# A streaming-encoder layer on eight cores: channel-major data, interleaved stages, streamed weights, shifted-stack convolution, pow on GpSimd, list scheduling

## The chip, the cores and the metric

The kernel runs on all 8 cores of one Trainium2 chip (two dies, cores 0 to 3 and 4 to 7). Each core does the same program on its own four prompt sequences and its own share of sample streams; no core waits for another. The metric is device time in microseconds (us) of the slowest core. TensorE is called PE, VectorE DVE, ScalarE ACT, GpSimd POOL and SyncE SP, as in the profile.

A program on all 8 cores has a second, slower state in some of its executions: one die (sometimes both) shows a lower granted clock and the time is some per cent longer.

## The reference, cut to what matters

```python
# D_MODEL 1024, 2048 tokens per prompt sequence, D_FF 2816 = 22*128, D_LRU = D_CONV = 512
def stream_layer(x, c, ...):
    sh1, sc1, gt1, ... = silu(c) @ w_ada + b_ada               # per-sequence modulation
    h = rms_norm(x, g1) * (1 + sc1) + sh1
    x = x + 0.5 * gt1 * ((silu(h @ wg1) * (h @ wu1)) @ wd1)    # FFN1
    h = rms_norm(x, g2) * (1 + sc2) + sh2
    z_lx, z_lg, z_cv, z_cg = split(h @ w_in)                   # 1024 -> 4 x 512
    # group A: width-4 causal conv, RG-LRU recurrence, GeLU gate
    y = causal_dwconv4(z_lx)
    r, i = sigmoid(blockdiag(y, wa)), sigmoid(blockdiag(y, wx))
    log_a = -8.0 * r * softplus(-lambda)
    a = exp(log_a)
    b = sqrt(-expm1(2 * log_a)) * (i * y)                      # sqrt(1 - a^2) * i * y
    lru = scan(h_t = a_t * h_{t-1} + b_t) * gelu(z_lg)
    # group B: GLU, depthwise conv of width 31, LayerNorm, SiLU
    v = silu(layer_norm(causal_dwconv31(z_cv * sigmoid(z_cg))))
    x = x + gt2 * (concat(rms_norm(lru), rms_norm(v)) @ w_out)
    h = rms_norm(x, g3) * (1 + sc3) + sh3
    x = x + 0.5 * gt3 * ((silu(h @ wg2) * (h @ wu2)) @ wd2)    # FFN2
    return rms_norm(x, final_g), states
```

Per core this is 16 tiles of 512 prompt tokens and one sample tile of 128 tokens.

The element-wise powers are a reciprocal square root for each of seven norms per tile (RMSNorm before each of three sub-layers, the LayerNorm, two group norms, the final norm), and, for each of four channel blocks of the recurrence, one exponential `a` and one square root.

## The kernel before

It has three phases, each over all tiles: FFN1 with its bf16 weights resident in SBUF, the mixer, FFN2 with its weights loaded once more. Tokens lie on partitions in the FFN input, so each tile is transposed on PE.

```python
def fe_normb(...):                       # norm of 128 tokens; tokens on partitions
    act.activation(out=xq, in_=xb, func=AF.Square, accum_out=stat[:, b])       # sum of squares
    act.activation(out=stat[:, 4+b], in_=stat[:, b], func=AF.Sqrt, scale=1/D, bias=eps)
    dve.reciprocal(out=stat[:, 8+b], in_=stat[:, 4+b])          # one value per token: [128, 1]
    dve.tensor_scalar(out=xq, in0=xb, scalar1=stat[:, 8+b], op0=ALU.mult)
# ... cut ...
for k in range(8): pe.transpose(out=PSB[..k..], in_=xq[..k..])                 # L547
# ... cut ...
for j in range(22):                                                            # FFN
    for k in range(8): pe.matmul(PS[gb], lhsT=Wg[:, k, j], rhs=hT[:, k])       # L660
    for k in range(8): pe.matmul(PS[ub], lhsT=Wu[:, k, j], rhs=hT[:, k])       # L664
# ... cut: SiLU on ACT, product on DVE; the down projection is L691 ...

# the mixer's recurrence, per channel block c of 128 channels, 512 tokens
act.activation(out=BD, in_=tr, func=AF.Exp, scale=der3, bias=der3)             # a
act.activation(out=BC, in_=tr, func=AF.Exp, scale=der2, bias=der2)             # a^2
act.activation(out=BC, in_=BC, func=AF.Sqrt, scale=-0.25, bias=0.25)           # sqrt(1 - a^2)/2
# the depthwise conv of width 31: 31 diagonal 128x128 matrices per channel block
for k in range(31):
    pe.matmul(PS[bank], lhsT=D31[:, c, k, :], rhs=CU[:, c, k:k+512])           # L1011
# the group norm
act.activation(out=RS, in_=PS[6], func=AF.Sqrt, scale=1/512, bias=4*eps)
dve.reciprocal(out=RS, in_=RS)
# ... cut ...
```

Of the kernel before, what the change touches and what calls it, by code (L numbers as in the profile page):

```python
# [16 lines left out]
SEQ = 2048  # L17
DSEQ = 32
PSEQ_PER_CORE = 4
SSEQ_PER_CORE = 4  # L20
NPT = PSEQ_PER_CORE * SEQ
NST = SSEQ_PER_CORE * DSEQ
NSEQ = 8
EPS = 1e-6
NT = 512

class _FakeIns:
    def then_inc(self, *a, **k):
        return self

# [9 lines left out]

def _fsz(ap):
    sh = ap.shape
    n = 1
    for d in sh[1:]:
        n *= int(d)
    return n

def _cost(eng, rec):
    name, a, kw = rec
    out = kw.get('out', a[0] if a else None)  # L50
    try:
        n = _fsz(out) if out is not None else 1
    except Exception:
        n = 1
    if name == 'dma_start':
        try:
            nbytes = out.size() * (2 if out.dtype == BF16 else 4)
        except Exception:
            nbytes = 1 << 16
        return 2500.0 + nbytes / 150.0  # L60
    if eng == 'pe':
        if name == 'transpose':
            return 160.0
        rhs = kw.get('rhs')
        nn = _fsz(rhs)
        mul = 4.0 if rhs.dtype == F32 else 1.0
        return max(nn, 64) / 2.4 * mul + 4.0
    if eng == 'act':
        return 230.0 + 0.96 * n + (190.0 if kw.get('accum_out') is not None else 0.0)
    if eng == 'dve':  # L70
        if name == 'reciprocal':
            return 100.0 + 6.1 * n
        if name == 'tensor_tensor_scan':
            return 70.0 + 2.0 * n
        if name in ('tensor_tensor', 'scalar_tensor_tensor'):
            return 70.0 + 1.3 * n
        if name == 'memset':
            return 60.0 + 0.5 * n
        return 60.0 + 1.0 * n
    if eng == 'pool':  # L80
        if name == 'tensor_tensor':
            return 100.0 + 2.4 * n
        if name == 'memset':
            return 100.0 + 1.0 * n
        return 100.0 + 3.5 * n
    return 30.0

def _tbl(rec):
    name, a, kw = rec
    if name != 'activation':  # L90
        return None
    f = kw.get('func')
    if f in (AF.Sqrt,):
        return 'sqrt'
    if f in (AF.Tanh, AF.Exp):
        return 'tanhexp'
    if f in (AF.Silu,):
        return 'silu'
    if f in (AF.Ln,):
        return 'ln'  # L100
    return None

class Sched:
    ENGS = ['pe', 'act', 'dve', 'pool', 'sp']
    WINDOW = 700

    def __init__(self):
        self.ops = []
        self.lastw = {}
        self.readers = {}  # L110
        self.region = 0
        self.reorder = {0: True}

    def barrier(self, reorder=True):
        self.region += 1
        self.reorder[self.region] = reorder

    def add(self, eng, fn, reads=(), writes=(), slot=None):
        idx = len(self.ops)
        deps = {}  # L120
        for r in reads:
            w = self.lastw.get(r)
            if w is not None:
                deps[w] = True
        for r in writes:
            w = self.lastw.get(r)
            if w is not None:
                deps.setdefault(w, False)
            for rd in self.readers.get(r, ()):
                deps.setdefault(rd, False)  # L130
        keep = []
        alld = []
        for d, raw in deps.items():
            o = self.ops[d]
            if o['region'] != self.region:
                continue
            alld.append(d)
            if o['slot'] is None and o['eng'] == eng and slot is None and eng == 'pe':
# [4 lines left out]
        rec = fk.rec  # L143
        op = dict(eng=eng, fn=fn, deps=keep, alld=alld, slot=slot, val=None, used=False, region=self.region,
                  cost=_cost(eng, rec), tbl=_tbl(rec), idx=idx)
# [10 lines left out]
    def schedule(self):  # L156
        ops = self.ops
        nreg = self.region + 1
        byreg = [[] for _ in range(nreg)]
        for o in ops:  # L160
            byreg[o['region']].append(o['idx'])
        order = {e: [] for e in self.ENGS}
        regend = []
        tfree = {e: 0.0 for e in self.ENGS}
        fin = {}
        lasttbl = [None]
        for r in range(nreg):
            ids = byreg[r]
            t0 = max(tfree.values()) if r > 0 else 0.0
            for e in self.ENGS:  # L170
                tfree[e] = max(tfree[e], t0)
            ndep = {i: len(ops[i]['alld']) for i in ids}
            users = {i: [] for i in ids}
            for i in ids:
                for d in ops[i]['alld']:
                    users[d].append(i)
            ready = {e: [] for e in self.ENGS}
            pos = 0
            done = set()
            for i in ids:  # L180
                if ndep[i] == 0:
                    ready[ops[i]['eng']].append(i)
            nsched = 0
            ntot = len(ids)
            strict = ['sp'] if self.reorder.get(r, True) else list(self.ENGS)
            elist = {e: [i for i in ids if ops[i]['eng'] == e] for e in strict}
            eptr = {e: 0 for e in strict}
            idpos = {i: k for k, i in enumerate(ids)}
            while nsched < ntot:
                while pos < ntot and ids[pos] in done:  # L190
                    pos += 1
                lim = ids[min(pos + self.WINDOW, ntot - 1)] if pos < ntot else 0
                best = None
                for e in self.ENGS:
                    lst = ready[e]
                    if not lst:
                        continue
                    cands = lst
                    if e in eptr:
                        el = elist[e]  # L200
                        while eptr[e] < len(el) and el[eptr[e]] in done:
                            eptr[e] += 1
                        if eptr[e] >= len(el) or el[eptr[e]] not in lst:
                            continue
                        cands = [el[eptr[e]]]
                    for i in cands:
                        if i > lim:
                            continue
                        o = ops[i]
                        st = tfree[e]  # L210
                        for d in o['alld']:
                            if fin[d] > st:
                                st = fin[d]
                        pen = 0.0
                        if e == 'act' and o['tbl'] is not None and lasttbl[0] is not None and o['tbl'] != lasttbl[0]:
                            pen = 1300.0
                        key = (st + pen, i)
                        if best is None or key < best[0]:
                            best = (key, i, st, pen)
                if best is None:  # L220
                    allr = [i for e in self.ENGS for i in ready[e]]
                    i = min(allr)
                    o = ops[i]
                    st = tfree[o['eng']]
                    for d in o['alld']:
                        st = max(st, fin[d])
                    best = ((st, i), i, st, 0.0)
                _, i, st, pen = best
                o = ops[i]
                e = o['eng']  # L230
                ready[e].remove(i)
                if o['slot'] is not None:
                    tfree[e] = st + 60.0
                    fin[i] = st + o['cost']
                else:
                    if e == 'act' and o['tbl'] is not None:
                        lasttbl[0] = o['tbl']
                    tfree[e] = st + pen + o['cost']
                    fin[i] = tfree[e] + (200.0 if e == 'pe' else 60.0)
                order[e].append(i)  # L240
                done.add(i)
                nsched += 1
                for u in users[i]:
                    ndep[u] -= 1
                    if ndep[u] == 0:
                        ready[ops[u]['eng']].append(u)
            regend.append({e: len(order[e]) for e in self.ENGS})
        self.order = order
        self.regend = regend
        self.makespan = max(tfree.values())  # L250

    def emit(self, nc, stack):
# [7 lines left out]
        nreg = len(self.regend)  # L260
        for r in range(nreg):
            for e in engs:
                lo = self.regend[r - 1][e] if r > 0 else 0
                hi = self.regend[r][e]
                for k in range(hi - 1, lo - 1, -1):
                    o = ops[order[e][k]]
                    if o['slot'] is None:
                        o['used'] = True
                        break
        cnt = {e: 0 for e in engs}  # L270
# [905 lines left out]
```

## Time and profile before

| | before |
|---|---|
| time, median of 4 fast runs | 6520.56 us (6518.27 to 6533.39) |
| busy share PE / DVE / ACT / POOL | 82% / 36% / 35% / 14% |
| PE per 512-token FFN tile | 124.5 us for 528 matmuls |
| mixer phase | about 2200 us |

The first fence is from the profile's page: busy us, share of the span and instructions of each engine; then the span in 40 equal slices with the busy share of each in tenths (9 is 90% or more) and the granted PE clock in tenths.

```profile
PE 5315.6 (82%) x25588; PEld 2434.9 (37%) x25588; DVE 2323.1 (36%) x3919; ACT 2311.6 (35%) x4040; POOL 917.2 (14%) x855
...
PE   3699999999999747657757766756999999999998
...
POOL 0100010010001122222222222221100100010010
PEclk7899999999999978878878877867999999999999
```

There are two plateaus of nines with a valley between them: the FFN phases keep PE full, the mixer phase does not. The next view cuts the span at the phase borders (range, length, busy us and instructions of PE, PE's weight loads, DVE, ACT, POOL, granted PE clock, busy share of the DMA engines, GB/s).

```profile
0.00:342.50 342.50, 180.81 (x801) 79.15 (x802) 63.90 (x155) 48.70 (x86) 47.55 (x63) 0.77 0.85 133
342.50:2218.00 1875.50, 1774.58 (x8360) 815.48 (x8359) 444.59 (x804) 455.96 (x799) 150.45 (x119) 0.96 0.15 51
2218.00:4420.00 2202.00, 1422.89 (x7066) 638.82 (x7064) 1223.04 (x1860) 1145.93 (x1893) 534.25 (x511) 0.79 0.16 53
4420.00:4587.00 167.00, 124.52 (x593) 58.29 (x594) 42.78 (x86) 51.78 (x99) 29.54 (x40) 0.85 0.88 158
4587.00:6519.00 1932.00, 1812.76 (x8772) 843.19 (x8770) 548.74 (x1015) 609.27 (x1163) 155.39 (x123) 0.96 0.15 51
```

In the third row no engine is full, PE is at 65% and DVE at 56%, which fits a mixer that waits for its own chain. The first and the fourth row are mostly weight loads, with the DMA engines at 0.85 and 0.88 and PE busy 53% and 75%. So the change has a fair target: fill the mixer's holes and the load times with FFN matmuls.

How fast PE runs is read from the timeline (start us, us, engine, line, operation, names, shapes, count, and in brackets the idle time before and what ended it).

```profile
342.48 1.89 PE L660 MATMUL ps<-hT,Wg 128*128 128x512 bf16 x8
344.21 1.89 PE L664 MATMUL ps<-hT,Wu 128*128 128x512 bf16 x8
...
418.45 0.61 PE L547 MATMUL ps<-identb,xnb_0 128*128 128x128 bf16 x8
418.90 0.61 PE L547 MATMUL ps<-identb,xnb_1 128*128 128x128 bf16 x8
423.23 1.01 PE L547 MATMUL ps<-identb,xnb_2 128*128 128x128 bf16 x8 [3.72 <-DVE hT L563]
```

From start to start, eight matmuls take 344.21 − 342.48 = 1.73 us, so 216 ns for each 128x512 matmul. (The duration in the second column includes the tail of the pipeline; take the distance of starts.)

### The profile page before, as it was taken

The page shows a single profiled execution, that of the slowest core. Times are in us where ns is not written, and L with a number is a line of the kernel's source. Part 1 is how long each engine was busy: PE and PEld are TensorE (multiplying, and loading weights), DVE is VectorE, ACT ScalarE, POOL GpSimd, SP SyncE. Part 2 cuts the span into 40 slices and gives each one's busy share as a digit, 9 for nine tenths or more (in the row PEclk, how much of TensorE's full clock was granted, in tenths as well). Part 3 has the DMA queues.
Part 4 walks back from the last instruction along what each step waited for, and adds up shares of the span by engine and source line. Part 5 has one row for each costly group of instructions (what it writes and reads, how often), then busy time and mean ns, then how long its engine had stood idle before and what let it go on. Part 6 is the DMA issues. An engine that isn't in the chain of part 4 may idle for free.

```text
span 6518.4 us, 79218 instructions; the slowest of 8 cores (6502.7 to 6518.4 us)
## 1 busy us (share of the span) xinstructions
PE 5315.6 (82%) x25588; PEld 2434.9 (37%) x25588; DVE 2323.1 (36%) x3919; ACT 2311.6 (35%) x4040; POOL 917.2 (14%) x855
## 2 busy tenths in 40 slices
PE   3699999999999747657757766756999999999998
PEld 1344444444444423323323322332444444444444
DVE  1222222222222245565555565552222222232222
ACT  0222212222222145555554554542333332333332
POOL 0100010010001122222222222221100100010010
PEclk7899999999999978878878877867999999999999
DMA  8811111111111121111111111108111111111111
GB/s 120 149 65 46 43 65 52 43 53 64 43 46 62 47 61 63 51 46 67 47 46 52 59 49 48 60 27 152 65 52 43 52 65 43 43 66 52 39 56 43
DMA packets 141438, 381.75 MB, mean 59 GB/s; under 512 B 12808, under 2 KB 55944, under 8 KB 141016
## 3 DMA queue, kind: packets, MB, share of 16 engines
q1 hardware_dynamic: 87432, 316.77, 14.1%
q0 software_dynamic: 53600, 59.91, 6.4%
q8 instruction: 213, 3.49, 0.2%
q14 instruction: 193, 1.58, 0.1%
HBM read 333.44 MB, written 103.09 MB: 67 GB/s over the span
## 4 chain that ended last, share of the span: by engine, by line
PE 75%; DVE 7%; ACT 6%; issue 5%; DMA 5%; POOL 0%; DVEq 0%; ACTq 0%; POOLq 0%; SPq 0%
PE ps L691 20%; PE ps L660 18%; PE ps L664 18%; PE ps L1011 7%; PE ps L885 6%; PE ps L1079 3%; ACT hT L558 2%; DMA wslab<-w_ada 2%; DVE hT L563 1%; PE ps L547 1%; ACT hTm L558 1%; DMA Wu<-wu 1%; DVE hTm L563 1%; DMA Wd<-wd 1%; DVE BE L1036 1%
## 5 line engine op out<-in xcount | busy, mean ns | idle before, releaser
L660 PE MATMUL ps<-hT,Wg 128*128 128x512 bf16 (+1 forms) x5984 | 1361.9, 371 | 20.5 <-DVE hT L563 14.0
L664 PE MATMUL ps<-hT,Wu 128*128 128x512 bf16 (+1 forms) x5984 | 1359.9, 370 | 0.0
L691 PE MATMUL ps<-Wd,aT 128*128 128x512 bf16 x5720 | 1303.5, 392 | 14.9 <-DVE tmp_0 L694 8.9
L691 PEld LDWEIGHTS ps<-Wd,aT 128*128 128x128 bf16 x5720 | 575.2, 101 | 730.2 <-issue 100.0
L660 PEld LDWEIGHTS ps<-hT,Wg 128*128 128x128 bf16 x5984 | 574.1, 98 | 688.2 <-issue 29.1
L664 PEld LDWEIGHTS ps<-hT,Wu 128*128 128x128 bf16 x5984 | 574.3, 98 | 666.1 <-issue 2.9
L885 PE MATMUL ps<-hTm,Win 128*128 128x512 bf16 (+1 forms) x2176 | 650.7, 389 | 134.8 <-DVE hTm L563 100.9
L668 ACT ACTIVATE sg_0<-ps 128x512 bf16<-128x512 f32 (+1 forms) x374 | 216.3, 578 | 1304.9 <-PE ps L660 1259.4
L1011 PE MATMUL ps<-CU,D 128*128 128x512 bf16 (+1 forms) x2480 | 591.5, 347 | 27.5 <-DVE CU L994 27.5
L671 DVE TENSOR_TENSOR aT<-ps,sg_1 128x512 bf16<-128x512 f32 (+1 forms) x374 | 249.9, 668 | 850.5 <-PE ps L660 748.2
L671 DVE TENSOR_TENSOR aT<-ps,sg_0 128x512 bf16<-128x512 f32 (+1 forms) x374 | 250.0, 668 | 834.1 <-PE ps L660 755.9
L668 ACT ACTIVATE sg_1<-ps 128x512 bf16<-128x512 f32 (+1 forms) x374 | 216.2, 578 | 811.7 <-PE ps L660 784.9
L697 POOL TENSOR_TENSOR xep_0<-xep_0,tmp_0 128x512 f32<-128x512 f32 x66 | 83.4, 1264 | 2938.2 <-DVE tmp_0 L694 2938.2
L885 PEld LDWEIGHTS ps<-hTm,Win 128*128 128x128 bf16 x2176 | 216.6, 102 | 400.4 <-issue 188.6
L558 ACT ACTIVATE hT<-ps,AB_B,AB_A 128x128 bf16<-128x128 bf16 (+1 forms) x544 | 246.4, 453 | 325.9 <-DVE hT L563 275.1
L1079 PE MATMUL ps<-Wout,MTm 128*128 128x512 bf16 x1040 | 315.8, 392 | 34.3 <-DVE tmpm L1082 20.1
L1011 PEld LDWEIGHTS ps<-CU,D 128*128 128x128 bf16 x2480 | 215.4, 100 | 269.8 <-issue 56.0
L563 DVE TENSOR_SCALAR hT<-ps,AB_A,AB_B 128x128 bf16<-128x128 bf16 (+1 forms) x544 | 185.5, 341 | 342.3 <-ACT hT L558 283.2
L1085 POOL TENSOR_TENSOR xepm<-xepm,tmpm 128x512 f32<-128x512 f32 x130 | 177.0, 1362 | 806.8 <-DVE tmpm L1082 756.1
L547 PE MATMUL ps<-identb,xnbm 128*128 128x128 bf16 x520 | 81.1, 282 | 171.4 <-DVE hTm L563 116.2
L901 DVE SCALAR_TENSOR_TENSOR BA<-LX,V5T,BA 128x512 f32<-128x512 f32 (+1 forms) x240 | 201.1, 838 | 15.7 <-DVE BA L901 1.1
L1047 PE MATMUL ps<-cb,ones 128*128 128x512 bf16 (+1 forms) x68 | 38.5, 566 | 186.1 <-ACT cb L1045 184.1
(192 smaller groups left out, 4533.1 us busy)
## 6 DMA issues: line engine op xcount, KB each, us to landing
xinm<-x1p SPq DMA_DIRECT2D x64, 512.0 KB, 3.3
xepm<-x1p SPq DMA_DIRECT2D x64, 512.0 KB, 3.3
x2p<-xepm SPq DMA_DIRECT2D x64, 512.0 KB, 2.7
wslab<-w_ada POOLq DMA_DIRECT2D x18, 1024.0 KB, 17.3
xin_0<-xp SPq DMA_DIRECT2D x32, 512.0 KB, 4.1
xin_1<-xp SPq DMA_DIRECT2D x32, 512.0 KB, 5.2
xep_0<-xp SPq DMA_DIRECT2D x32, 512.0 KB, 4.3
xep_1<-xp SPq DMA_DIRECT2D x32, 512.0 KB, 4.4
```

Of the source, the lines that this page charges most:

```text
L558: S.add('act', lambda e, k=k, s=s, lo=lo, hi=hi, pl=pl, bank=bank: e.activation(out=hT[:, k, lo:hi], in_=PSB[bank][:, pl:pl + hi - lo], fu ...
L563: S.add('dve', lambda e, k=k, s=s, lo=lo, hi=hi, pl=pl, bank=bank: e.tensor_scalar(out=hT[:, k, lo:hi], in0=PSB[bank][:, pl:pl + hi - lo], ...
L660: S.add('pe', lambda e, j=j, k=k, gb=gb, nt=nt: e.matmul(PS[gb][:, 0:nt], lhsT=Wg[:, k, j * 128:(j + 1) * 128], rhs=hT[:, k, 0:nt], start= ...
L664: S.add('pe', lambda e, j=j, k=k, ub=ub, nt=nt: e.matmul(PS[ub][:, 0:nt], lhsT=Wu[:, k, j * 128:(j + 1) * 128], rhs=hT[:, k, 0:nt], start= ...
L668: S.add('act', lambda e, gb=gb, sgi=sgi, nt=nt: e.activation(out=sg[sgi][:, 0:nt], in_=PS[gb][:, 0:nt], func=AF.Silu), reads=['ps%d' % gb] ...
L671: S.add('dve', lambda e, j=j, ub=ub, sgi=sgi, nt=nt: e.tensor_tensor(out=aT[:, j, 0:nt], in0=PS[ub][:, 0:nt], in1=sg[sgi][:, 0:nt], op=ALU ...
L691: S.add('pe', lambda e, j=j, b=b, n=n, yb=yb: e.matmul(PS[yb][:, :], lhsT=aT[:, j, b * 128:(b + 1) * 128], rhs=Wd[:, j, n * 512:(n + 1) * ...
L885: add('pe', lambda e, m=m, k=k, bank=bank: e.matmul(PS[bank][:, 0:nt], lhsT=Win[:, k, m * 128:(m + 1) * 128], rhs=hT[:, k, 0:nt], start=(k ...
L901: la('dve', lambda e, c=c, c0=c0, L=L, lxo=lxo, k=k: e.scalar_tensor_tensor(out=BA[:, c, c0:c0 + L], in0=LX[:, c, lxo + k:lxo + k + L], sc ...
L1011: ca('pe', lambda e, c=c, k=k, bank=bank, c0=c0, L=L, cuo=cuo: e.matmul(PS[bank][:, c0:c0 + L], lhsT=D31[:, c, k, :], rhs=CU[:, c, cuo + k ...
L1079: S.add('pe', lambda e, k=k, b=b, n=n, yb_=yb_: e.matmul(PS[yb_][:, :], lhsT=MT[:, k, b * 128:(b + 1) * 128], rhs=Wout[:, k, n * 512:(n + ...
L1085: S.add('pool', lambda e, n=n, xe=xe: e.tensor_tensor(out=xe[:, n * 512:(n + 1) * 512], in0=xe[:, n * 512:(n + 1) * 512], in1=tmp[0][:], o ...
```

## The change: its intent, and the diff

The intent: keep PE in dense matmuls all the time. The data are channel-major from the start, so that nothing is transposed. FFN1, mixer and FFN2 of different tiles are emitted together and a list scheduler with a table of costs fixes each engine's order. Since FFN1 and FFN2 run side by side, their weights no longer fit: they are streamed as bf16 through a ring of six buffers for every tile. The conv becomes 128 matmuls of 32 output columns per tile, in four column groups of the PE array. And with channels on partitions a norm's statistic is no longer one value per partition but a whole 128x512 tile, made by a ones-matmul in fp32.

The change also moves every power off ACT. Before, ACT switched between function tables (SiLU and tanh in one, Exp and Sqrt in others): the trace of before has 327 table loads of 1283 ns. After, `pow` runs on POOL, and only 3 table loads are left.

```diff
-    act.activation(out=BD, in_=tr, func=AF.Exp, scale=der3, bias=der3)
-    act.activation(out=BC, in_=BC, func=AF.Sqrt, scale=-0.25, bias=0.25)
-    act.activation(out=RS, in_=PS[6], func=AF.Sqrt, ...); dve.reciprocal(RS, RS)
+    def ppow(out, in0, in1, nt, reads, writes):
+        st = 128                                          # pieces of 128 columns
+        for a in range(0, nt, st):
+            ...
+            tt(out[:, a:b], i0, i1, ALU.pow, reads, writes, eng='pool')
+    def rstd(nt, ac, act_, ones, rd, rdt, eps, bank):     # all RMS norms; whole 128 x nt tiles
+        mm(PS[bank][:, 0:nt], ones[:], ac[:, 0:nt], ...)  # fp32 ones-matmul
+        tsc1(rd[:, 0:nt], PS[bank][:, 0:nt], eps, ALU.add, ...)
+        ppow(rd, rd, cst[:, 0:1], nt, ...)                # ** -0.5
+    # ... cut; in the recurrence, per channel block:
+    tsc1(TR[:, 0:nt], TR[:, 0:nt], 1.0, ALU.add, ...)
+    ppow(TR, der[:, c, 2:3], TR, nt, ...)                 # a = base ** (tanh + 1)
+    actf(MM[:, 0:nt], TR[:, 0:nt], AF.Square, ...)
+    tsc(MM[:, 0:nt], MM[:, 0:nt], -0.25, 0.25, ALU.mult, ALU.add, ...)
+    ppow(MM, MM, cst[:, 1:2], nt, ...)                    # ** 0.5
```

That is 15 powers per prompt tile (7 norms, 4 channel blocks with 2 each), in four pieces: 60 instructions per tile, and 15 for the sample tile, 975 in all. The other parts, cut to their core:

```diff
-    for k in range(31): pe.matmul(PS[bank], lhsT=D31[:, c, k, :], rhs=CU[..])
+    for i in range(4):                                    # stack of 4 shifted copies of 32 channels,
+        dma(ssv[32*i:32*i+32, ...], dc[:, 3-i: ...])      # made through DRAM
+    for m in range(8):
+        for g in range(4):                                # four column groups of 32
+            mm(PS[bc][32*g:32*g+32, 0:nt], Wcv[:, 4*c+g, m, :], rhs, m == 0, m == 7, ...)
+ # weights of each tile from a ring of 6 (first tile: fp32 load, cast on DVE, bf16 written back)
+    dma(ring[r][:, 0:n], dstb[i, :, :], [tag], [rt], 'rl%d' % r)
+ # the scheduler's table of costs (ns; n = columns)
+    if m == 32:                      return max(nn, 64) / 2.33 / 3.0     # a conv matmul
+    if name == 'tensor_tensor' and op == ALU.pow:  return 200.0 + 10.0 * n    # on POOL
+ # order of emission: FFN1 runs 5 tiles ahead; a mixer stands beside the FFNs before its own FFN2
+    ffn = [(1, t) for t in tiles[:lead]]                  # lead = 5
+    for b in range(NTILES):
+        if lead + b < NTILES: ffn.append((1, tiles[lead + b]))
+        ffn.append((2, tiles[b]))
# ... cut ...
```

## The prediction

> **What bounds it now.** The stage table (busy time by stretch): preparation and first weights 0-342 us; first FFN to about 2250; mixer to about 4430; second FFN with its weight load to 6518. In both FFNs TensorE (PE) is the limit: busy about 95%, granted clock 0.96. The timeline shows dense runs at 215.8 ns per 128x512 matmul (eight take 1.726 us). One 512-token FFN tile takes 124.5 us: 528 matmuls are 114 us, the rest is the 8 us transpose patch, where PE waits for evictions of hT (458 ns ACT, 344 ns DVE each). Neither can shrink much. The mixer is not PE-bound: PE 64%, DVE 55%, ACT 52%, POOL 24%, clock 0.79. It takes 2180 us, about 134 us per tile, while its matmuls (340 full-width, 32 transposes) need 76 us. So about 1000 us go to mixer latency and about 600 us to weight loads at phase borders (DMA share 0.8 there, PE half idle).
>
> **What the change does.** It removes all transposes (data come channel-major), the phase borders, and 124 diagonal conv matmuls per tile, for 128 of 32 output columns in four column groups. It mixes FFN1, mixer and FFN2 of different tiles so that PE always has FFN work. It adds: weights streamed as bf16 for every tile, about eight fp32 ones-matmuls per tile, pow on POOL, and the conv stacks through DRAM.
>
> **PE per prompt tile.** 1056+128+64+8 = 1256 matmuls at 215.8 ns: 271 us. Conv: the Trainium skill (TensorE: Matmul & The Clock Gate, Part 3) has three column tiles at 2.38x; taking three times, 128 x 72 ns = 9 us; nothing in this trace shows it. fp32 at four passes: 7 us. Sum 287 us, x16 = 4600; sample tile 80.
>
> **The rest, per 287 us.** From durations here (DVE 0.67-0.97 us, ACT 0.6-0.7, POOL 1.3-1.4 per 128x512): DVE about 125 us, ACT 105, POOL 150 (half of it pow, for which I have only the change's own scheduling table, 6 us per 512). None binds if this holds. DMA: about 63 MB per tile, 218 GB/s; here 65 GB/s cost a 0.19 share, so about 0.64. Tight in bursts, the six-deep ring absorbs it. SP: about 175 issues of 0.32 us, 56 us.
>
> **Exposed.** Start (modulation weights, first tile's weights in fp32): about 110 us. End: with lead 5 the last five FFN2s have no FFN1 beside them; the mixer's chain (norm 32, four recurrences of 25 each with two pows, layer norm and output norms 35, output 20, next norm 35: about 220 us estimated) is longer than the PE work beside it (165): about 200 us lost. Final norm 30. Steady stalls 2%: 100.
>
> 4600+80+110+200+30+100 = 5120; for order mismatches between the static list order and the chip I say **5150 us**, range 4900 to 5500. Chances: faster 0.95, same 0.03, slower 0.02.
>
> **What would show it.** PE over 90% busy from about 150 us to the last 800; 215.8 ns per matmul still; clock near 0.97; transposes gone; conv's four groups overlapping (about 70 ns each); DMA share 0.6-0.7; POOL about 50%; PE idle late, in the last five tiles, behind the mixer's chain (waits on POOL pow, DVE hM). First 110 us DMA-bound.
>
> **What would make it wrong.** (1) Clock: the same page (Part 1) has a 13/16 limit for dense matmul on three or more cores of a die; this trace disagrees (0.96-0.98, all eight cores dense), but the change loads every engine at once; a chronic 0.81 would give about 6000. (2) pow twice as slow: POOL near 230 us per tile, the mixer's chain near 330: stalls throughout and a longer tail. (3) DMA unable to hold 220 GB/s with eight cores: PE waits for the ring. (4) Column groups not overlapping: +300. (5) In-order waits of PE on late mixer operands: several per cent.

## The result, and the profile after

| | before | after |
|---|---|---|
| time, median of 4 fast runs | 6520.56 us | 24725.15 us (24633.54 to 24770.66) |
| after over before | | 3.789 (95% interval 3.780 to 3.798) |
| PE / DVE / ACT / POOL busy | 82% / 36% / 35% / 14% | 26% / 9% / 6% / 86% |

A ratio is the mean time of one kernel's fast runs over that of the other's in the same rounds, so it is not quite the ratio of the medians. The record notes no error of the outputs. The predicted 5150 us was wrong by a factor of 4.8, and in the other direction from the time before.

The page of after, the same rows as above:

```profile
PE 6513.0 (26%) x24376; PEld 2502.8 (10%) x24376; DVE 2162.1 (9%) x3457; ACT 1599.5 (6%) x2760; POOL 21308.4 (86%) x2103
...
PE   4440122222222323213232322323231221121212
...
POOL 5459999989899797997979899797979889898986
PEclk7665555565665666556565655656565665565656
```

The plateaus of nines have moved from PE to POOL. One stretch in the middle, as in the table of stages before:

```profile
5000.00:10000.00 5000.00, 1376.80 (x4845) 518.63 (x4842) 421.27 (x617) 334.76 (x547) 4419.07 (x414) 0.61 0.14 44
```

POOL is busy 4419 of 5000 us with only 414 instructions: more than 10 us each. The granted clock of 0.61 belongs to a PE that is idle most of the time; in the first experiment, which makes PE busy again, it is 0.94. The four costliest groups that do powers, from the page's part 5 (busy us, mean ns of one, idle time before and what ended it):

```profile
L423 POOL TENSOR_TENSOR LT<-der,LT 128x128 f32<-128x128 f32 x260 | 5401.1, 20774 | 734.9 <-DVE LT L430 420.5
L423 POOL TENSOR_TENSOR rdM<-rdM,cst 128x128 f32<-128x128 f32 x260 | 5387.7, 20724 | 142.9 <-DVE rdM L430 132.0
L423 POOL TENSOR_TENSOR LT<-LT,cst 128x128 f32<-128x128 f32 x260 | 5392.0, 20738 | 87.4 <-DVE LT L426 47.6
...
L423 POOL TENSOR_TENSOR rdF<-rdF,cst 128x128 f32<-128x128 f32 x195 | 4047.5, 20756 | 131.1 <-DVE rdF L430 123.9
```

These are the 975 pow instructions: decay, mixer norms, square roots, FFN norms. Together they take 20,228 us, 20.75 us each. The change's own table, from which I took the number, has 200 + 10 × 128 = 1480 ns. It is off by a factor of 14.

The chain of waits that ended last, by engine, and two of the longest waits (us in total, times, longest):

```profile
POOL 59%; issue 26%; PE 10%; DMA 2%; DVE 1%; ACT 1%; another core or an unknown queue 0%; POOLq 0%; SPq 0%; DVEq 0%; ACTq 0%
```

```profile
ACT LT L416 <- POOL LT L423: 4691.5, 68, 142.3
...
PE ps L440 <- POOL acM L423: 3212.6, 70, 137.2
```

The second wait is not for a power: `acM` is the sum of squares that POOL adds up at about 1.3 us apiece. The timeline of POOL, and then of PE at the same time, shows how such a sum comes to wait (here `acF`, the same sum of an FFN's norm):

```profile
9989.84 20.72 POOL L423 TENSOR_TENSOR LT<-LT,cst 128x128 f32<-128x128 f32 x1 [1.40 <-DVE LT L426]
10010.52 1.26 POOL L423 TENSOR_TENSOR acF<-acF,sqF 128x512 f32<-128x512 f32 x1
10011.74 41.59 POOL L423 TENSOR_TENSOR LT<-LT,cst 128x128 f32<-128x128 f32 x2
10053.29 1.26 POOL L423 TENSOR_TENSOR acF<-acF,sqF 128x512 f32<-128x512 f32 x1
```

```profile
10011.93 2.04 PE L440 MATMUL ps<-acF,onesD 128*128 128x512 f32 x2 [95.91 <-POOL acF L423]
```

POOL does its queue in order. The scheduler had laid one cheap addition between two power pieces, believing each to last 1.5 us. Each addition now stands behind 20.7 us or more: the one that ended at 10011.78 us released a PE that had been idle for 96 us.

### The profile page after: what moved, and what is told of

Its sections match the earlier page's. It is cut to its first block, busy times and chain, and to the rows that moved or that the text cites. A ratio compares the mean times of both kernels' runs of the same rounds, so it can differ in the third digit from the quotient of the medians.

```text
span 24755.9 us, 80999 instructions; the slowest of 8 cores (24518.5 to 24755.9 us)
## 1 busy us (share of the span) xinstructions
PE 6513.0 (26%) x24376; PEld 2502.8 (10%) x24376; DVE 2162.1 (9%) x3457; ACT 1599.5 (6%) x2760; POOL 21308.4 (86%) x2103
## 4 chain that ended last, share of the span: by engine, by line
POOL 59%; issue 26%; PE 10%; DMA 2%; DVE 1%; ACT 1%; another core or an unknown queue 0%; POOLq 0%; SPq 0%; DVEq 0%; ACTq 0%
POOL LT L423 37%; POOL rdM L423 14%; PE ps L440 10%; POOL rdF L423 7%; POOL acF L423 1%; DMA rsM<-x1p 0%; POOL acM L423 0%; ACT LT L416 0%; DMA ring<-wgub 0%; DMA x2p<-rsM 0%; DMA LT<-w_ada 0%; DVE LT L722 0%; DMA SS<-cud 0%; DVE uF L419 0%
## 5 line engine op out<-in xcount | busy, mean ns | idle before, releaser
L423 POOL TENSOR_TENSOR LT<-der,LT 128x128 f32<-128x128 f32 x260 | 5401.1, 20774 | 734.9 <-DVE LT L430 420.5
L423 POOL TENSOR_TENSOR rdM<-rdM,cst 128x128 f32<-128x128 f32 x260 | 5387.7, 20724 | 142.9 <-DVE rdM L430 132.0
L423 POOL TENSOR_TENSOR LT<-LT,cst 128x128 f32<-128x128 f32 x260 | 5392.0, 20738 | 87.4 <-DVE LT L426 47.6
L440 PE MATMUL ps<-hF,ring 128*128 128x512 bf16 (+1 forms) x11968 | 3408.2, 417 | 3358.6 <-ACT sg L416 1421.0
L423 POOL TENSOR_TENSOR rdF<-rdF,cst 128x128 f32<-128x128 f32 x195 | 4047.5, 20756 | 131.1 <-DVE rdF L430 123.9
L440 PE MATMUL ps<-hM,mring 128*128 128x512 bf16 (+1 forms) x3264 | 1243.1, 450 | 8890.0 <-ACT LT L416 2641.6
L440 PEld LDWEIGHTS ps<-hF,ring 128*128 128x128 bf16 x11968 | 1242.3, 107 | 5218.6 <-issue 4674.2
L440 PE MATMUL ps<-aT,ring 128*128 128x512 bf16 (+1 forms) x5984 | 1639.8, 415 | 463.5 <-DVE rsF L419 292.5
L423 POOL TENSOR_TENSOR acF<-acF,sqF 128x512 f32<-128x512 f32 (+1 forms) x357 | 444.4, 1245 | 597.7 <-ACT sqF L416 571.6
L440 PE MATMUL ps<-SS,Wcv 128*32 128x512 bf16 (+1 forms) x2176 | 813.0, 404 | 152.1 <-DMA SS<-cud 149.2
L440 PEld LDWEIGHTS ps<-aT,ring 128*128 128x128 bf16 x5984 | 626.6, 107 | 1356.7 <-issue 1106.8
```

The source lines that it names most:

```text
L423: return S.add(eng, lambda e: e.tensor_tensor(out=out, in0=in0, in1=in1, op=op), reads=reads, writes=writes)
L440: return S.add('pe', lambda e: e.matmul(out, lhsT=lhsT, rhs=rhs, start=start, stop=stop), reads=reads, writes=writes)
```

## The experiments

The theories, in words. The first: the price of pow explains the whole miss; at the assumed price the kernel would take about 5150 us. The rivals: POOL or its order binds even at the assumed price (C in the quoted texts, where letters are working names); or there is a second, smaller mistake hidden behind the first. When the second turned out to be true, three more theories followed: conv matmuls alternate with full-width matmuls and each change costs PE time (E); the start is bound by DMA traffic in the background (H); the tail is set by the mixers being placed too late (T). For the price of pow itself: a cost per column (J), against a cost per instruction (K), contention with VectorE (L), or a cost that depends on the values (M), the partitions or the output type. Runs of one group below shared a chip and the runs of before on it (spread5_again had its own).

### First group: take the pow away, in three sizes, and replace it

Before's fast runs of this group: 6516.25, 6518.72 and 6524.75 us.

**pow_off.** Its output is wrong, which doesn't matter for the time. Each pow becomes one ordinary operation on the same 128 columns; the cost that the scheduler sees is kept, so the order of every queue is identical.

```diff
-            tt(out[:, a:b], i0, i1, ALU.pow, reads, writes, eng='pool')
+            op = ALU.subtract if 'der' in reads else ALU.mult
+            S.add('pool', <tensor_tensor with op>, ..., cost=200.0 + 10.0 * (b - a))
```

> Wrong result on purpose: every pow on POOL becomes one mult or subtract on the same 128 columns; the order of every queue is the same as in the changed kernel. Theory A (only pow is mis-sized: 975 pows of 20.7 us each are 20.2 ms of POOL, all the rest of the prediction stands): about 4900 to 5200 us, POOL about 25 to 30% busy, PE clock back near 0.95. Rival B (the structure itself is slow: static order, weights streamed, conv stacks through DRAM, and pow only hides it): still above 6500 us.

Measured: 6430.23 and 6423.48 us in fast runs, ratio to before 0.9855 (0.9812 to 0.9897; the record's verdict is "unclear"). So the pow accounts for 24725 − 6427 = 18.3 ms, nearly all of the miss. But 6427 is also 1277 us above the prediction, and the expected 4900 to 5200 was missed: the first theory is not the whole story.

```profile
PE 5589.1 (87%) x24376; PEld 2308.3 (36%) x24376; DVE 2200.6 (34%) x3457; ACT 1601.7 (25%) x2760; POOL 1564.6 (24%) x2103
```

PE now is the full engine, with 5589 us busy where I had counted on some 4700. The surplus lies on PE itself. The timeline of a steady stretch shows it:

```profile
3006.38 1.24 PE L440 MATMUL ps<-hF,ring 128*128 128x512 bf16 x5
3007.56 0.39 PE L440 MATMUL ps<-SS,Wcv 128*32 128x512 bf16 x1
3007.88 0.39 PE L440 MATMUL ps<-hF,ring 128*128 128x512 bf16 x1
3008.20 0.39 PE L440 MATMUL ps<-SS,Wcv 128*32 128x512 bf16 x1
3008.52 0.39 PE L440 MATMUL ps<-hF,ring 128*128 128x512 bf16 x1
```

Conv matmuls (`SS,Wcv`, 32 columns) and FFN matmuls alternate one by one here, and every start is 0.32 us after the last: a pair takes 0.641 us where I had 0.216 + 0.072 = 0.288. Over 128 pairs in each of 16 tiles the surplus is 0.353 × 2048 = 723 us. This became theory E. The scheduler makes the pattern itself: its model ends a PE operation 200 ns after its last cycle, conv matmuls into the same bank depend on each other, so after each it finds the next conv "not ready" and puts an FFN matmul between. Running the change's scheduler again off the chip confirms this: as it stands, 1973 of its 2176 conv matmuls stand alone; with the 200 ns set to zero, all of them stand in blocks of 32.

**pow_as_priced.** Its output is wrong, which doesn't matter for the time. Each piece becomes one 512-column operation of about 1.26 us, close to the assumed 1.48. The queue orders are again identical.

```diff
-            tt(out[:, a:b], i0, i1, ALU.pow, ...)
+            S.add('pool', <tensor_tensor over [:, 0:nt], mult or subtract>, ..., cost=200.0 + 10.0 * min(st, nt))
```

> Wrong result on purpose: each pow becomes one mult or subtract over all 512 columns, about 1.26 us, near the 1.48 us for which the change's scheduling table charges a pow; same order of every queue. Theory A: this is the kernel that I predicted, so 5150 us within 250, with a tail of some 200 us where PE waits in the last five tiles. Rival B: above 6500 us. Rival C (POOL would bind even at the table's price): POOL over 80% busy and about 6000 us.

Measured: one fast run, 6512.54 us; the profiled run was slow (6873.9 us), with POOL at 32%. So with a pow at nearly its assumed price the kernel is still over 1300 us above 5150, and only 86 us above pow_off. POOL does not bind at that price; rival C falls. The expected 5150 within 250 was missed, and rival B (something else in the structure is slow) comes nearest; the second group shows what it is. With a single fast run the 86 us are rough, but the gap to 5150 does not depend on that.

**pow_norms_only.** Its output is wrong, which doesn't matter for the time. The recurrence's 520 pow pieces are replaced as in pow_off, the norms' 455 stay.

> Wrong result on purpose: the 520 pows of the recurrence (two of three groups) become mult or subtract; the 455 pows of the norms stay. Theory A: POOL time adds up: 455 x 20.74 us = 9.4 ms plus 1.2 ms of other POOL work, and some idle: 11 to 13 ms. Rival D (the recurrence's serial chain is what costs, the norms' pows are hidden): close to the time with no pow at all, under 7 ms.

Measured: one run, fast, 15128.21 us, POOL 71% busy. The expected 11 to 13 ms was missed. But the parts add up almost without overlap: 455 × 20.75 us = 9.44 ms of POOL time bring 15128 − 6427 = 8.70 ms, and the recurrence's 520 × 20.75 = 10.79 ms bring 24725 − 15128 = 9.60 ms. Both kinds cost about 0.9 us per us of POOL, so neither is hidden behind other work and rival D falls.

**lnexp.** Correct. Every pow goes back to ACT, as Exp(p · Ln(x)), with the decay as one Exp of the tanh. "ScalarE: Activation LUTs" of the Trainium skill, section "Table sets: the hidden batching unit", has `ln` and `exp` in one set, `natural_log_exp_and_others`, so this needs one switch of tables where Exp and Sqrt would need two (in spread5_again's trace an Ln at 3010.16 us and its Exp at 3010.94 us have no load between them); the scheduler charges 1283 ns for a switch.

```diff
-        ppow(rd, rd, cst[:, 0:1], nt, ...)
+        actf(rd[:, 0:nt], PS[bank][:, 0:nt], AF.Ln, ..., bias=eps)
+        actf(rd[:, 0:nt], rd[:, 0:nt], AF.Exp, ..., scale=-0.5)
-            ppow(TR, der[:, c, 2:3], TR, nt, ...)
+            actf(TR[:, 0:nt], TR[:, 0:nt], AF.Exp, ..., scale=der[:, c, 2:3], bias=der[:, c, 2:3])
```

> Right result: every pow is made on ACT as Ln and Exp, one table set of their own, and the recurrence's decay as Exp; the scheduling table charges 1.28 us for each change of table set. Theory A: about 5000 to 5300 us (ACT grows from 100 to about 170 us per tile, still below PE's 287), results within tolerance, faster than the kernel before. Rival B: above 6500 us.

Measured: fast runs 6559.63 and 6533.23 us, ratio to before 1.0038 (0.9949 to 1.0127; verdict "unclear"). The expected 5000 to 5300 was missed for the reason that pow_off had just shown. But it is a correct kernel with the pow gone: of 24.7 ms, 18.2 went by changing where 15 functions per tile are computed. Its price on ACT, from the groups of lnexp:

```profile
L425 ACT ACT_TABLE_LOAD x494 | 633.8, 1283 | 946.9 <-PE ps L449 874.1
```

634 us of table loads, on an engine that is 38% busy with them. The change had avoided them at a cost of 20.2 ms on POOL.

Two builds that gave no run belong here: pow on VectorE was refused by the compiler in both forms that I tried, `tensor_tensor` and `tensor_scalar`. So VectorE was no way out here, and no run shows its price.

### Second group: conv matmuls in one block

Before's fast runs: 6529.27 and 6530.77 us.

**convrun_off.** pow_off with the 32 conv matmuls of a channel block given to the scheduler as one operation, so that nothing comes between them.

```diff
-            for m in range(8):
-                for g in range(4):
-                    mm(o, Wcv[:, 4*c+g, m, :], rhs, m == 0, m == 7, ...)
+            S.add('pe', <all 32 matmuls>, reads=['Wcv', sst], writes=['ps%d' % bc],
+                  cost=32 * max(nt, 64) / 2.33 / 3.0)
```

> Wrong result on purpose: pow_off, and the 32 matmuls of one conv chunk are issued as one block, so that no FFN matmul stands between two of them. In pow_off they alternate with FFN matmuls one by one, and each of the two then takes 320 ns (a pair 641 ns). Theory E ([...]within a block four column groups overlap): conv at about 72 ns, 128 x (641 - 216 - 72) ns x 16 tiles = 720 us less, so about 5700 us. Rival F (column groups never overlap, but the change of mode is what cost the rest): conv at 216 ns, 430 us less, about 6000. Rival G (a 32-column matmul takes 320 ns by itself): 215 us less, about 6200.

Measured: no run fast on both dies; the lowest 5932.94 us, slow, with die 0, the undisturbed one, at 5740 to 5761 us. In the profile of pow_off, whose dies were both undisturbed, die 0 took 6400 to 6428 us: some 660 us less. Since the other die was slowed, this is a hint; the next run decides.

**convrun.** The same edit on lnexp, so correct.

> Right result: lnexp with the conv matmuls as blocks of 32. Theory E: about 5800 us, 11% under the kernel before; rival F about 6100; rival G about 6300.

Measured: fast runs 5839.93 and 5823.18 us, ratio to before 0.893 (0.8875 to 0.8986; two fast runs of each, and the record's verdict is "unclear"). Between lnexp and convrun (means of fast runs, different chips with before at about 6520 and 6530) lie 6546 − 5832 = 715 us, against the 723 us computed from the alternating pairs. The conv group of pow_off, then that of convrun, and three lines of convrun's timeline, with two blocks:

```profile
L440 PE MATMUL ps<-SS,Wcv 128*32 128x512 bf16 x2048 | 762.4, 395 | 42.1 <-DMA SS<-cud 39.3 <-ACT LT L416 2.8
```

```profile
L755 PE MATMUL ps<-SS,Wcv 128*32 128x512 bf16 x2048 | 150.0, 444 | 126.7 <-DMA SS<-cud 125.9 <-ACT LT L425 0.8
```

```profile
3032.77 2.65 PE L755 MATMUL ps<-SS,Wcv 128*32 128x512 bf16 x32 [3.38 <-DMA SS<-cud]
...
3099.98 1.91 PE L755 MATMUL ps<-SS,Wcv 128*32 128x512 bf16 x32 [2.33 <-DMA SS<-cud]
3101.82 0.39 PE L449 MATMUL ps<-hM,mring 128*128 128x512 bf16 x1
```

The mean duration of one hardly changes (395, 444 ns) because it includes the tail of the pipeline, but the busy time falls from 762.4 to 150.0 us: 73 ns for each matmul on average, against 216 ns of a full-width one.

This average mixes two kinds of block. In 42 of the 64 blocks of this core the granted clock was 1.0 throughout. There the four column groups start within about 10 ns, and the next four 0.216 us later, so a conv matmul takes 0.216 / 4 = 54 ns; the second block above is one of these, 1.84 us to the next full-width matmul. In the other 22, such as the first above, the granted clock was 0.5 to 0.87, and at 0.5 four take 0.43 us. All 22 came after PE had been idle for more than 2 us, and none of the 36 blocks after a shorter pause was slow. "TensorE: Matmul & The Clock Gate", Part 3, has 2.38 times for three column tiles; here four give 216 / 54 = 4 times at full clock. So the 72 ns of the prediction agree with the average partly by luck: it had assumed threefold overlap, and the trace has fourfold overlap and a lower clock in a third of the blocks.

**convrun_halfbg.** convrun, with the background work of the start (casts of later weights, later modulation chunks) issued at every second step.

```diff
-            if bg is not None:
+            if bg is not None and j % 2 == 0:
```

> Right result: convrun, and the background weight casts and modulation chunks are issued at every second hidden block instead of every one, so over 5 FFN stages in place of 2.5. Theory H (the first 1000 us are bound by DMA, at a share of 0.8 to 0.99, because casts and streamed weights fall together): 100 to 250 us less than convrun. Rival I (streaming and the first fp32 weights alone fill the DMA then): within 50 us of convrun.

Measured: one fast run, 5701.92 us, 130 us below convrun's mean. Theory H holds as far as one run can show. From 320 to 640 us PE was busy 251 us in convrun and 296 us here (read from the two traces; the second line is not shown).

**pow_micro.** convrun with pow instructions of several sizes and kinds appended on POOL, after everything else; correct, one fast run of 6589.95 us, of which the appended work is the last 740.

```diff
+    pw(acF, 16, ...); pw(acF, 32, ...); pw(acF, 64, ...); pw(acF, 128, ...); pw(acF, 256, ...); pw(acF, 512, ...)
+    # 128 columns: other exponents, base of ones-tile, bf16 output, 32 partitions; a mult for comparison
```

> convrun with pows appended after the last work, when VectorE is idle: 16 to 512 columns, other exponents, a base of one value, 32 partitions, bf16 out. Theory J[...]: time proportional to columns, 162 ns each: 16 columns 2.6 us, 512 columns 83 us; the same for every exponent, and the same 20.7 us for 128 columns with VectorE idle. Rival K (a fixed cost per instruction, so that narrow pieces were the mistake): 512 columns near 21 us. Rival L (contention with VectorE[...]): well under 20.7 us here. Rival M (time depends on the values): exponents 1 and 2 or the constant base much faster.

Measured, from the groups by shape (busy us, mean ns of one):

```profile
L432 POOL TENSOR_TENSOR acF<-sqM,cst 128x512 f32<-128x512 f32 x3 | 245.7, 81915 | 0.3
...
L432 POOL TENSOR_TENSOR acF<-sqM,cst 128x128 f32<-128x128 f32 x3 | 62.2, 20723 | 0.3
...
L432 POOL TENSOR_TENSOR rsF<-onesD,cst 128x128 f32<-128x128 f32 x3 | 62.2, 20718 | 0.0
...
L432 POOL TENSOR_TENSOR acF<-sqM,cst 128x16 f32<-128x16 f32 x3 | 8.7, 2896 | 0.1
...
L432 POOL TENSOR_TENSOR LX<-sqM,cst 128x128 f32<-128x128 f32 x3 | 1.2, 408 | 0.0
```

From 16 to 512 columns the time grows by (81915 − 2896) / 496 = 159 ns per column, with about 0.3 us fixed. Exponents −0.5, 0.5 and others, a constant base (`onesD`), a bf16 output and 32 partitions all took 20.72 us for 128 columns. It is a price per column and nothing else that was varied, which is what theory J expected. VectorE was busy only 3.6 us of the last 740, so contention with it (L) is not the cause. The multiplication of the same 128 columns (last line) took 408 ns, 51 times less. So a different piece size, or fewer partitions, would not have helped the change. Fewer columns would: a norm of 512 tokens has 512 different statistics, repeated on 128 partitions here. Laid out as 128 x 4 they would take an estimated 0.3 + 4 × 0.159 = 1 us by these figures; no run tried it. "GPSIMD Engine Reference" of the Trainium skill, section 4.1, sends element-wise work to VectorE because POOL is about 2 times slower there. For such operations the trace of after agrees: the subtraction (POOL) and the multiplication (DVE) of `BE` and `rdM`, 128x512 each, took 1.26 and 0.68 us (medians). But that factor is for add, multiply and max, and the page has no price for pow.

### Third group: how the switch costs, and the tail

Before's fast runs: 6523.33, 6523.04 and 6526.24 us.

**conv4.** lnexp, with conv given to the scheduler in blocks of four matmuls, one for each column group, instead of 32. If the cost lies in the change between the two kinds, 8 blocks per channel block make a quarter as many changes as the alternation of 32 singles.

```diff
+            for m in range(8):
+                S.add('pe', <the 4 matmuls of m>, ..., cost=4 * max(nt, 64) / 2.33 / 3.0)
```

> Right result: lnexp with the conv matmuls as blocks of four (the four column groups of one tap group), and other matmuls between the blocks. Theory E (the loss is paid per change between column-tile width, about 0.35 us for going there and back: 641 - 216 - 72 ns): 32 blocks instead of 128 per tile, so three quarters of convrun's gain of about 700 us: about 5950 to 6050 us, 120 to 200 us above convrun. Rival N (overlap needs long runs; four in a row gain little): near lnexp, 6400 or more.

Measured: fast runs 5940.02, 5916.08 and 5921.85 us, ratio 0.9083 (0.9052 to 0.9114): a little below the expected 5950 to 6050, and between lnexp and convrun as theory E needs.

```profile
3049.35 0.40 PE L755 MATMUL ps<-SS,Wcv 128*32 128x512 bf16 x4
3049.68 0.39 PE L449 MATMUL ps<-hM,mring 128*128 128x512 bf16 x1
3050.00 0.40 PE L755 MATMUL ps<-SS,Wcv 128*32 128x512 bf16 x4
```

A block of four conv matmuls takes 0.33 us from start to start, the same as a single one did in pow_off, and the full-width matmul between two blocks takes 0.32 us instead of 0.216. So the four column groups do overlap, as long as nothing stands between them, and the alternation costs two things. A lone conv matmul takes as long as a group of four, a whole pass of 0.216 us, and about 0.105 us is added at each change of kind: 0.641 = 2 × 0.216 + 2 × 0.105. Over 2048 pairs, the first is (0.216 − 0.054) × 2048 = 332 us and the second 0.21 × 2048 = 430 us, 762 together. convrun gives back 13 us for its own 128 changes and about 25 us for its blocks at a lower clock, which leaves some 725; 715 was measured. No run has a lone conv matmul without a change beside it, so the split is read from the starts. But conv4 and convrun differ mainly in the number of changes, 16 against 2 in each of 64 channel blocks, and (5926 − 5832) / (14 × 64) = 0.105 us again.

For conv4 the starts give a channel block of 8 × 0.65 + 24 × 0.216 = 10.4 us, against 32 × 0.641 = 20.5 in lnexp; times 64 channel blocks that is 648 us less, and 6546 − 5926 = 620 was measured (means of fast runs, different chips).

"TensorEngine Tiling (Array Packing)" of the Trainium skill, Key Properties, says: "Mode switching requires drain". This trace agrees and puts a number on it. That a drain is what happens inside is the page's statement; the runs show only the time, and that it goes with the number of changes.

**spread5.** convrun_halfbg, with the mixers' place in the emission order changed. In the change a mixer stands just before its own FFN2, so the last five tiles have a mixer and an FFN2 each and no FFN1 to fill. Here the mixers start earlier and are spaced by 1.5 FFNs.

```diff
-        i = pos2[b-1] - (1 if ffn[pos2[b-1]-1][0] == 1 else 0) if b > 0 else pos2[0] - 2
-        i = max(i, pos1[b] + 1, 2)
+        i = min(max(4 + int(1.5 * b), pos1[b] + 1), pos2[b] - 2)
```

> Right result: convrun_halfbg with the mixer of tile b placed at stage 4 + 1.5 b (but after its first FFN), so that all mixers are placed before the last FFN stages, where convrun_halfbg has one mixer beside each of the last five second FFNs and a stage takes 230 us. Theory T (those stages wait for the mixer's chain): a last stage falls to about 125 us, some of it paid earlier where mixers add 50 us of matmuls: 150 to 280 us less than convrun_halfbg, 5420 to 5550 us. Rival: the last stages are slow for another reason (norm chain of the FFN itself, DMA): less than 60 us.

Measured: one fast run, 5511.18 us. The time between the output stores of successive tiles in the tail was 230 us in convrun_halfbg (4705.74 to 5626.20 us over four tiles) and is 126 us here (4946.53 to 5451.20 over four). That is 191 us less in total than convrun_halfbg's one fast run (5701.92 us, another chip), within the expected 150 to 280. Three stretches of convrun, then of spread5 (start, steady, tail); the start differs because spread5 has convrun_halfbg's slower casts too:

```profile
320.00:640.00 320.00, 250.78 (x1187) 110.64 (x1210) 74.93 (x131) 52.49 (x82) 36.26 (x51) 0.88 0.97 228
1500.00:4602.00 3102.00, 2908.47 (x13748) 1283.43 (x14018) 1212.01 (x1656) 1505.05 (x2167) 669.21 (x609) 0.98 0.66 202
4602.00:5840.00 1238.00, 928.46 (x5180) 437.84 (x5263) 492.13 (x888) 580.11 (x935) 261.57 (x299) 0.88 0.56 175
```

```profile
320.00:640.00 320.00, 293.04 (x1451) 133.51 (x1479) 87.82 (x151) 65.27 (x103) 32.31 (x44) 0.98 0.95 251
...
2058.00:4732.00 2674.00, 2472.56 (x11881) 1087.08 (x12112) 1098.48 (x1531) 1463.52 (x2068) 637.25 (x590) 0.98 0.65 201
4732.00:5510.00 778.00, 691.72 (x3964) 345.11 (x4028) 284.88 (x610) 296.31 (x539) 121.14 (x159) 0.96 0.66 212
```

The last row of each is the tail: PE 75% busy in convrun, 89% in spread5, and 460 us shorter, part of which is work moved to the middle. (About 2% of the matmul records are missing from these two traces, as the smaller count of matmuls than of weight loads shows, so PE is a little busier than they say.) Theory T holds.

**spread7.** spread5 with FFN1 seven tiles ahead, casts at every third step and mixers at 1.4.

> Right result: as spread5, with a lead of 7 first FFNs and background casts at every third hidden block, mixers at 5 + 1.4 b. If the first 1000 us are bound by the bytes to be moved there, another 50 to 150 us less than spread5; if the longer run of FFN1 alone only moves the same bytes, no difference.

Measured: fast runs 5604.31 and 5587.71 us, ratio 0.8577 (0.8547 to 0.8608). Slower than spread5 by some 85 us, where I had expected 50 to 150 us less or none. Three things were changed at once, so the run does not tell which of them hurt. Its trace shows where: from 320 to 640 us PE is busier (318 us against 293 in spread5_again), but from 640 to 2058 us it is busy 1147 us against 1219.

**spread5_again.** The same kernel as spread5, in five rounds, against six fast runs of before of its own (6519.18 to 6531.71 us).

> The same kernel as spread5, for a verdict against the kernel before from more fast runs: 5500 us within 30, ratio 0.84 to 0.85.

Measured: fast runs 5492.13, 5489.55, 5494.32 and 5480.10 us, ratio to before 0.8415 (0.8403 to 0.8428). This is the best correct kernel, 15.9% less time than before.

```profile
PE 4866.8 (89%) x24376; PEld 2162.6 (39%) x24376; DVE 2137.6 (39%) x3223; ACT 2566.5 (47%) x3757; POOL 1138.1 (21%) x1128
```

## Why the prediction was wrong, point by point

The step that failed is this one, as the prediction put it: "POOL 150 (half of it pow, for which I have only the change's own scheduling table, 6 us per 512). None binds if this holds." I took 5.9 us for 512 columns from the change's table; the trace has 4 × 20.75 = 83 us, and 15 of those per tile are 1245 us of POOL against the 287 us of PE that I called the limit. The 24.7 ms are 16.25 tiles of this (975 × 20.75 us = 20.2 ms), POOL's other 1.1 ms, and the waits in which POOL had nothing ready. The prediction did name this as its second risk, but only as "twice as slow"; nothing supported a factor of two more than one of fourteen. No trace of mine had a pow in it, and the number came from the author of the change, whose order of instructions is built on the same error. So the range should have been far wider, or the chance of "slower" far above 0.02.

With pow taken out, the other terms of the sum can be judged one by one:

| term of the prediction | predicted | measured | verdict |
|---|---|---|---|
| full-width matmul | 215.8 ns | 216 ns in dense runs of the variants | held |
| pow, 128 columns on POOL | 1.48 us | 20.75 us | failed: +18.3 ms |
| fp32 ones-matmuls | four passes, 7 us per tile | 0.85 us each from start to start (convrun_halfbg, 3047.67 to 3048.52), 3.9 times 0.216 | held |
| conv matmul | 72 ns | in blocks 54 ns at full clock, 73 on average; pairs of 641 ns in the change's order | held for the unit partly by luck, failed for the order: about +715 us |
| DMA share, steady | 0.64 at 218 GB/s | 0.66 at 202 GB/s (convrun) | held |
| DVE per tile | 125 us | 2162 us / 16.25 = 133 us | held |
| ACT per tile | 105 us | 1599 us / 16.25 = 98 us | held |
| clock | near 0.97, feared 0.81 | 0.98 in the steady stretches of fast runs; 0.81 for long stretches of a slow one | held in fast runs |
| start | 110 us of load | DMA share 0.90 or more to 640 us, 0.73 to 1500 us (convrun_halfbg) | too small |
| tail | 200 us lost | 230 us per tile against 165 us of estimated PE work, over four tiles about 260 us | held, a little small |
| PE over 90% in the middle | yes | 2908 of 3102 us, 94% (convrun) | held, once pow and conv were mended |

The prediction listed "Column groups not overlapping: +300" as a risk. That part came true, at about 332 us, though not for the reason I had feared: the hardware does overlap them, but the scheduled order hardly ever lets four stand together. The other 430 us, the changes of kind, I had not thought of at all. Neither is visible in the diff as a line; both follow from the 200 ns of latency in the scheduler's model, as the run of the scheduler without it shows.

The gain that I had described was there, but smaller: overlapping FFN and mixer, with the start and tail mended, brings 6520 to 5490 us. That still is 340 us above the 5150 that I said for the kernel without any mending. The start is the largest known part (PE 1679 us busy in the first 2058 us of spread5); its exact split between the volume of traffic and the order of the queue stays open, since spread7 did not tell them apart. In the steady stretch 6 to 7% of PE's time is lost to small waits, of which the conv's for its stacks through DRAM is one of the largest (126 us over all of convrun).

## What to carry to other kernels

A cost that no trace of yours contains is a hole in the prediction, and a number from the code under study does not fill it: multiply the instruction count by the worst price you can defend, and if the answer changes sides, measure one instruction by itself before building a schedule on it. When one engine's busy row is full of nines, read its count as well as its time: 975 instructions at 20.75 us are a different disease from 10,000 at 2. And after removing the dominant cost, compare again with the number you had expected, because a second error of 1.3 ms was invisible behind one of 18.

For PE: keep matmuls of different column widths in blocks. A static order that alternates them one by one can cost more than twice what the matmuls cost in blocks (0.641 against 0.270 us for a pair here). And see that the data of a block are there when it starts: a third of convrun's blocks ran at a lower clock after a wait.

## What the Trainium skill lacked or had wrong

- "GPSIMD Engine Reference" has no price for pow in `tensor_tensor`. Measured: about 159 ns per column and 0.3 us fixed (20.72 us for 128 columns, 81.9 us for 512), the same for all exponents, for 32 partitions and for a bf16 output; a multiplication of the same 128 columns takes 0.41 us. The page's factor of about 2 against VectorE is for add, multiply and max and says nothing of it.
- No page that I found says which engines take pow. POOL ran 975 of them in `tensor_tensor`, at 20.75 us each. VectorE was refused in `tensor_scalar` and in `tensor_tensor`, and POOL in `tensor_scalar`, before any run.
- "TensorEngine Tiling (Array Packing)", Key Properties, names the drain at a change of mode but gives no cost. Measured: about 0.105 us for each change between matmuls of 32 and of 128 output columns, so that an alternating pair takes 0.641 us, where the same two take 0.216 + 0.054 = 0.270 us in blocks at full clock.
- "TensorE: Matmul & The Clock Gate", Part 3, lists three column tiles (2.38 times) and not four. Measured here for four: 54 ns per matmul against 216, 4 times, at a granted clock of 1.0.
- The same page, Part 1, has a 13/16 clock limit for dense matmuls on three or more cores of a die, to be budgeted for. With all eight cores dense the fast runs had a granted clock of 0.96 to 0.98 in before and 0.98 in the variants' steady stretches; lower clocks came only in slow runs or where PE was partly idle. The page's figure does appear there: in pow_as_priced's slow profile, core 6 stood at 0.81 in every 150 us slice from 1500 to 3300 us and at 0.99 or 1.00 from 3450 to 5100 us, with PE over 90% busy in both. So the runs show 13/16 as a state that comes and goes, not as the rule for dense work on all cores.
- "ScalarE: Activation LUTs", "What ACT_TABLE_LOAD costs", has about 2.7 us for a switch: a load of 1283 ns and a drain of 1380 ns. The load took 1283 ns here too, but an activation that followed a load at 3031.99 us in spread5_again started at 3033.28, and the load had begun 0.08 us after the end of the activation before it: the switch added about 1.4 us, nearer to the 1283 ns of the page "ScalarE activation tables: per-element evaluation and per-set limits". Its list of sets also lacks the one that holds SiLU with tanh, which this kernel uses without a load between them (3 loads in all of after).
